# First projection in blocks of 2, 2, 4 and 8 k tiles, with the modulation placed anew

## The chip, the cores and the metric

One NeuronCore of a Trainium2 chip runs the kernel alone. TensorE (PE) multiplies matrices and holds its sums in PSUM, VectorE (DVE) and ScalarE (ACT) compute element by element, GpSimd (POOL) has little to do here, and SyncE (SP) issues most transfers from memory. The metric is the device time of one execution in microseconds.

## The reference

Two layers over 256 tokens of 2048 channels: layer 0 is gated linear attention (GLA), layer 1 a diagonal state-space mixer (S5). Each layer is modulated by a vector c, and its input is normalised after the residual:

```
mod = silu(c) @ ada_w + ada_b            # per layer: shift, scale, gate (2048 each)
u   = x * (1 + scale) + shift
# GLA
proj = u @ w_in                          # 2048 x (1024 q + 1024 k + 4096 v + 4096 z + 16 gate)
q, k, v, z, g = split(proj)
# per chunk of 64 tokens: state = decay * state + k_dec^T v ; o = q state
y = rmsnorm(o) * silu(z) ; h = y @ w_out
x = layernorm(alpha * x + (1 + gate) * h)
# S5: proj, per-group linear recurrence, gelu, GLU with a 4096 x 4096 matrix, output projection
```

All is float32. The change lies in the first projection (q, k and v of layer 0) and in the shift and scale of layer 0 that it needs.

## The kernel before

Channels are cut into 16 k tiles of 128. Each float32 product is made of three matmuls: weights are split into hi (a cast on ScalarE, L145) and lo (weight minus hi, on VectorE, L146), the input u likewise, and hi·hi, lo·hi and hi·lo are summed in PSUM (L167 to L169 for v, L180 to L182 for q and k).

The first projection can't begin with all 16 k tiles, since u needs shift and scale of the k tiles that it uses, and these are products of c with `ada_w` that have still to be loaded. So it runs over blocks of k tiles. In a block, `vqk_steps` (L366 to L401) takes a step for each column group of 512 (8 groups of v, 4 of q and k) and each pair of k tiles: load 512 KB of weights (`wload`, L136), `split`, then 12 matmuls of 128x512 for v or 24 of 128x256 for q and k. When a column group has all k tiles of the block, its sums leave PSUM: in block 0 by copies on ScalarE (L385, L399), later by additions on VectorE into `vbig` (L383) or `qk` (L397). The last block does q and k first. The four blocks have 2, 4, 4 and 6 k tiles: 12, 24, 24 and 36 steps.

A name such as lov33 is the lo of v, column group 3, k pair 3 (k tiles 6 and 7); v160 is the PSUM bank of group 1 in the block that begins at k tile 6, tokens 0 to 127.

Weights lie in a ring of 4 tiles and 2 borrowed ones, hi and lo in rings of 3. The transfers of weights, of modulation pieces and of x are all issued from SP's queue, in the order of the program.

Beside the steps runs other work, put there by a table (`put`, `put_ada`, `put_u`, L743 to L778): after step i of block n it issues the pieces listed for (n, i). A modulation piece `put_ada(part, k0, nk, dve, ...)` makes shift (part 0) or scale (part 1) of nk k tiles from k0: 4 loads of 1 MB for nk = 4, 4 groups of products, either on TensorE (`psa`, L272: 16 products) or, where dve is true, on VectorE (`row`, L264 and L266: 16 multiply-adds over 128 nk columns), and at the end small products that turn the row into columns (`psmod`, L236) and one VectorE operation that adds the bias (`mods`, L239 or L241). `put_u` transposes two k tiles of x on TensorE (`psx`, L357) and makes u from them (`uf`, `u0h`, `u0l`). Where the program orders it after a step, each piece is told to be issued after that step's lo and last matmul.

In block 2, a generator `lam` also computes the S5 layer's powers in small VectorE operations (`lamst`, `pwr`, `pwt`, `crci`), one portion a step, and `prep_small` fills a DRAM tensor with zeros (`dk<-zt`, L458). Powers are turned on TensorE (`psl`) and copied by ScalarE (`l8`, L574). In the last block, `pump(V_RATE)` runs a background list of tasks for layer 1's modulation and preparation, V_RATE tasks a step on average, and from step GATE_AT on the gate of the GLA is computed (`gla_gate`).

Before the first block, the head computes shift and scale for block 0's two k tiles at once (`ada_now`, L281 to L288). The order on each engine is set by a scheduler that takes these issue conditions and its own estimate of durations; the kernel does not write it out.

Of the kernel before, what the change touches and what calls it, by code (L numbers as in the profile page):

```python
# [16 lines left out]
D = 2048  # L17
# [16 lines left out]
def trunk(ctx, tc, x, c, ln_g, ln_b, ada_w, ada_b, gla_w_in, gla_gate_w2, gla_gate_b, gla_norm_g,  # L34
# [39 lines left out]
    def s8t(name, shape, dt=F32):  # L74
        return s8.tile([P] + shape, dt, tag="s8", name=name)
# [20 lines left out]
    def pump(rate=1.0):  # L96
        pace[0] += rate
        while pace[0] >= 1.0:
            pace[0] -= 1.0
            if bg:  # L100
                bg.pop(0)()
# [178 lines left out]

    def ada_now(*a, rows=None, between=None):  # L281
        loads, mults, fin = ada_pe(*a, rows=rows)
        for f_ in loads + mults[:-1]:
            f_()
        if between:
            between()
        mults[-1]()
        return fin  # L288

    gate_dst = [None, None]  # L290
# [45 lines left out]
    def x_load(c0, c1):  # L336
        if not xr:
            xr.extend([s8t(f"xrow{i}", [D]) for i in range(2)])
        for tt in range(2):
            dma(xr[tt][:, c0:c1], x[0, tt * P:(tt + 1) * P, c0:c1])  # L340
# [11 lines left out]
    def u_tr(k2):  # L352
        ps = psx(f"psx{k2}")
        for kk in range(2):
            for tt in range(2):
                k = k2 + kk
                PE.transpose(ps[:, kk * T + tt * P:kk * T + (tt + 1) * P], xr[tt][:, k * P:(k + 1) * P], ident)  # L357
        return ps

    def u_fin(k2, ps):  # L360
        for kk in range(2):
            k = k2 + kk
            uf = tp.tile([P, T], F32, tag="uf", name=f"uf{k}", bufs=2)
            V.tensor_scalar(uf, ps[:, kk * T:(kk + 1) * T], mods[:, 0, 1, k:k + 1], mods[:, 0, 0, k:k + 1], op0=ALU.mult, op1=ALU.add)
            hilo(u0.hi(k), u0.lo(k), uf)
# [42 lines left out]
    def vectors():  # L408
# [8 lines left out]
        S.copy(vt, ps[:, :104])  # L417

    ada0 = ada_now(0, 0, 0, 2)

    vr2 = tp.tile([64, P], F32, tag="vr2", name="vr2", bufs=1)
# [4 lines left out]
    PE.transpose(ps[:, :64], vr2, ident[:64, :64])  # L426
    S.copy(abT, ps[:, :64])

    blocks = ((0, 2), (2, 4), (6, 4), (10, 6))
    ada0()  # L430
    x_load(0, 256)
    early = more(2, 0)

    got = []
    ada_now(0, 1, *blocks[0], rows=[8, 4, 4], between=lambda: got.append(u_tr(0)))()
    u_fin(0, got[0])

# [222 lines left out]
    for part in range(2):  # L660
        for j in range(4):
            bg.extend(ada_dve(1, part, j))
    V_RATE, Z_RATE, OP_RATE = 0.825, 0.944, 0.755
    KEEP = (4, 6)
    GATE_AT = 15
    SCAN_RATE = 1.728
    Y_RATE = 2.311
    qt, kt = qk
# [77 lines left out]
    def put(n, i, f_):  # L746
        along.setdefault((n, i), []).append(f_)

    def put_ada(part, k0, nk, dve, at_load, at_mult, at_fin):
        loads, mults, fin = ada_pe(0, part, k0, nk, dve)  # L750
        for f_, at in zip(loads + mults + [fin], at_load + at_mult + [at_fin]):
            put(*at, f_)

    def put_u(k2, at_tr, at_fin):
        got = []
        put(*at_tr, lambda: got.append(u_tr(k2)))
        put(*at_fin, lambda: u_fin(k2, got[0]))

    def at(n, *i):
        return [(n, j) for j in i]  # L760

    put(0, 0, lambda: x_load(256, 768))
    put_ada(1, 2, 4, True, at(0, 0, 1, 2, 3), at(0, 1, 2, 3, 4), (0, 6))
    put_ada(0, 2, 4, False, at(0, 4, 5, 6, 7), at(0, 6, 6, 8, 8), (0, 9))
    put_u(2, (0, 10), (0, 10))
    put_u(4, (0, 11), (0, 11))
    put(1, 2, vectors)
    put_ada(1, 6, 4, True, at(1, 0, 2, 4, 6), at(1, 1, 3, 5, 7), (1, 9))
    put(1, 7, lambda: x_load(768, D))
    put_ada(0, 6, 4, False, at(1, 8, 10, 12, 14), at(1, 11, 11, 15, 15), (1, 17))  # L770
    put_u(6, (1, 19), (1, 19))
    put_u(8, (1, 21), (1, 21))
    put_ada(0, 10, 4, False, at(1, 16, 18, 20, 22), at(2, 0, 0, 2, 2), (2, 4))
    put_ada(1, 10, 4, False, at(2, 0, 2, 4, 6), at(2, 4, 4, 8, 8), (2, 10))
    put_ada(0, 14, 2, False, at(2, 8, 10), at(2, 12, 12), (2, 14))
    put_ada(1, 14, 2, False, at(2, 12, 14), at(2, 16, 16), (2, 18))
    for i, k2 in enumerate((10, 12, 14)):
        put_u(k2, (2, 19 + i), (2, 19 + i))  # L778

    for n, blk in enumerate(blocks):  # L780
        steps = vqk_steps(*blk)
        for i, f_ in enumerate(steps):
# [8 lines left out]
            elif n == 3:  # L791
                pump(V_RATE)
                if i >= GATE_AT:
                    next(gate, None)
# [89 lines left out]
    for g in range(8):  # L884
# [9 lines left out]
        for f in range(4):  # L894
            i = (g * 4 + f) % 8
# [354 lines left out]
    for g in range(8):  # L1250
# [9 lines left out]
        for f in range(4):  # L1260
            i = (g * 4 + f) % 8
# [43 lines left out]
    for g in range(8):  # L1305
# [14 lines left out]
        for f in range(4):  # L1320
            i = g * 4 + f
# [112 lines left out]
```

## Time and profile before

| | |
|---|---|
| median of 3 runs | 1849.08 us (1848.76 to 1849.77) |
| the profiled execution | 1845.55 us, span 1843.8 us, mean granted clock 0.994 |
| busy: TensorE / its weight loads | 1793.7 us (97%) / 1587.9 us (86%) |
| busy: VectorE / ScalarE / GpSimd | 1426.4 (77%) / 898.7 (49%) / 68.1 us (4%) |
| first projection, blocks 0 to 3 start at | 21.2, 76.1, 154.5, 241.2 us; it ends at 366.6 us |

The profile's times are from the start of the span. In lists of groups and instructions, "out<-in" names the tiles written and read; what stands in brackets, or behind a bar, is the idle time of the engine before the instruction and what ended it.

### The profile page before, as it was taken

Reading aid. Unit: us, or ns where it says so; the run is one execution under the profiler, and the core shown is the slowest. Engines: PE = TensorE matmul, PEld = TensorE weight load, DVE = VectorE, ACT = ScalarE, POOL = GpSimd, SP = SyncE. Lnnn points to the kernel's source line nnn. Section 1 sums busy time; section 2 is a strip of 40 time slices with the busy share of each in tenths; the row PEclk is TensorE's granted clock in tenths of the full one; section 3 lists DMA queues with packets and bytes.
Section 4 is the critical chain, followed back from the end, with each engine's and each line's share of the span. In section 5 each row is a group of like instructions: output and inputs, shape, how many; then the busy total and the mean of one; then the engine's idle time right before and its main releaser. Section 6 shows DMA issues by size and latency. Waiting matters only on the chain.

```text
span 1843.8 us, 33865 instructions
## 1 busy us (share of the span) xinstructions
PE 1793.7 (97%) x13619; PEld 1587.9 (86%) x13619; DVE 1426.4 (77%) x1890; ACT 898.7 (49%) x1252; POOL 68.1 (4%) x76
## 2 busy tenths in 40 slices
PE   6999999999999999999999999999999999999997
PEld 4777798799999888799999999989888888888885
DVE  4667875989999988697899789889677775557556
ACT  3533465655556333654544544545544544444332
POOL 0000000000000000002123210000000000000000
PEclk9999999999999999999999999999999999999999
DMA  9887976789889998575655477999688886668653
GB/s 354 321 319 251 326 230 213 219 296 325 285 277 325 336 353 287 172 221 158 178 156 150 138 211 213 240 246 249 223 275 268 274 277 208 190 192 326 193 184 92
DMA packets 244182, 449.48 MB, mean 244 GB/s; under 512 B 19540, under 2 KB 49678, under 8 KB 242742
## 3 DMA queue, kind: packets, MB, share of 16 engines
q1 hardware_dynamic: 240088, 437.86, 74.1%
q0 software_dynamic: 3168, 8.41, 1.6%
q8 instruction: 107, 1.75, 0.4%
q10 hardware_dynamic: 768, 1.05, 0.2%
q14 instruction: 51, 0.42, 0.1%
HBM read 432.81 MB, written 14.42 MB: 243 GB/s over the span
## 4 chain that ended last, share of the span: by engine, by line
PE 85%; DVE 8%; DMA 2%; ACT 2%; issue 2%; SPq 0%; DVEq 0%; ACTq 0%
PE gl L192 13%; PE gl L193 6%; PE op L168 6%; PE op L167 6%; PE op L169 6%; PE z L182 3%; PE z L180 3%; PE z L181 3%; PE sz L180 3%; PE v L168 3%; PE sz L181 3%; PE sz L182 3%; PE v L169 3%; PE v L167 3%; PE su L180 2%; PE su L182 2%
## 5 line engine op out<-in xcount | busy, mean ns | idle before, releaser
L146 DVE TENSOR_TENSOR logl<-wgl,higl 128x1024 fp32r<-128x1024 f32 x128 | 156.5, 1224 | 113.2 <-ACT higl L145 109.7
L145 ACT CAST higl<-wgl 128x1024 fp32r<-128x1024 f32 x128 | 134.5, 1052 | 170.0 <-PE gl L192 160.9
L192 PE MATMUL gl<-yp,higl 128*128 128x512 f32 x512 | 178.4, 393 | 0.1
L192 PE MATMUL gl<-yb,higl 128*128 128x512 f32 x512 | 178.3, 393 | 0.0
L145 ACT CAST hio<-wo 128x1024 fp32r<-128x1024 f32 x96 | 101.3, 1055 | 155.7 <-PE op L169 142.8
L146 DVE TENSOR_TENSOR loo<-wo,hio 128x1024 fp32r<-128x1024 f32 x96 | 117.3, 1223 | 65.0 <-ACT hio L145 63.0
L309 DVE SCALAR_TENSOR_TENSOR acc<-wa,cs,acc 128x512 f32<-128x512 f32 x215 | 160.5, 747 | 2.7
L180 PE MATMUL su<-u1h,hisu 128*128 128x256 f32 x512 | 153.4, 301 | 1.8 <-DVE vv L1082 1.8
L180 PE MATMUL sz<-u1h,hisz 128*128 128x256 f32 x512 | 149.7, 292 | 1.2 <-ACT zs L1264 1.2
L180 PE MATMUL z<-u0h,hiz 128*128 128x256 f32 x512 | 148.7, 290 | 0.0
L182 PE MATMUL su<-u1h,losu 128*128 128x256 f32 x512 | 145.6, 285 | 0.4 <-DVE losu L146 0.4
L182 PE MATMUL z<-u0h,loz 128*128 128x256 f32 x512 | 145.0, 283 | 0.9 <-DVE loz L146 0.9
L181 PE MATMUL su<-u1l,hisu 128*128 128x256 f32 x512 | 145.8, 285 | 0.0
L182 PE MATMUL sz<-u1h,losz 128*128 128x256 f32 x512 | 144.8, 283 | 0.2 <-DVE losz L146 0.2
L181 PE MATMUL sz<-u1l,hisz 128*128 128x256 f32 x512 | 144.7, 283 | 0.0
L181 PE MATMUL z<-u0l,hiz 128*128 128x256 f32 x512 | 144.7, 283 | 0.0
L193 PE MATMUL gl<-yb,logl 128*128 128x256 f32 x512 | 142.8, 279 | 0.0
L193 PE MATMUL gl<-yp,logl 128*128 128x256 f32 x512 | 141.6, 279 | 0.0
L145 ACT CAST hisz<-wsz 128x1024 fp32r<-128x1024 f32 x64 | 66.9, 1050 | 103.7 <-PE sz L181 58.3
L192 PEld LDWEIGHTS gl<-yp,higl 128*128 128x128 f32 x512 | 95.8, 187 | 22.1 <-issue 0.8
L192 PEld LDWEIGHTS gl<-yb,higl 128*128 128x128 f32 x512 | 95.9, 187 | 21.9
L145 ACT CAST hisu<-wsu 128x1024 fp32r<-128x1024 f32 x64 | 66.7, 1050 | 94.8 <-PE su L181 70.0
(321 smaller groups left out, 5022.5 us busy)
## 6 DMA issues: line engine op xcount, KB each, us to landing
wgl<-in_s_w_glu SPq DMA_DIRECT2D x128, 512.0 KB, 4.7
wa<-in_ada_w SPq DMA_DIRECT2D x115, 512.0 KB, 5.1
wv<-in_gla_w_in SPq DMA_DIRECT2D x64, 512.0 KB, 6.5
wz<-in_gla_w_in SPq DMA_DIRECT2D x64, 512.0 KB, 5.1
wsu<-in_s_w_in SPq DMA_DIRECT2D x64, 512.0 KB, 3.7
wsz<-in_s_w_in SPq DMA_DIRECT2D x64, 512.0 KB, 4.7
wo<-in_s_w_out SPq DMA_DIRECT2D x64, 512.0 KB, 4.6
a<-in_ada_w SPq DMA_DIRECT2D x31, 1024.0 KB, 9.7
```

The costliest lines, as they stand in the source:

```text
L145: S.copy(hi, w)
L146: last_lo[0] = V.tensor_tensor(lo, w, hi.bitcast(F32), op=ALU.subtract).ins
L167: PE.matmul(banks[tt], lhsT=uh, rhs=hi[:, kk, :], start=(k == first), stop=False)
L168: PE.matmul(banks[tt], lhsT=uh, rhs=lo[:, kk, :], start=False, stop=False)
L169: last_mm[0] = PE.matmul(banks[tt], lhsT=ul, rhs=hi[:, kk, :], start=False, stop=(k == last)).ins
L180: PE.matmul(o, lhsT=wh, rhs=u.hi(k), start=(k == first), stop=False)
L181: PE.matmul(o, lhsT=wh, rhs=u.lo(k), start=False, stop=False)
L182: last_mm[0] = PE.matmul(o, lhsT=wl, rhs=u.hi(k), start=False, stop=(k == last)).ins
L192: PE.matmul(banks[f], lhsT=hi[:, kk, fs], rhs=u.both(k), start=(k == 0), stop=False)
L193: PE.matmul(banks[f][:, :T], lhsT=lo[:, kk, fs], rhs=u.hi(k), start=False, stop=(k == last))
L309: V.scalar_tensor_tensor(acc[0], w[:, kk, :], cs[:, k:k + 1], acc[0], op0=ALU.mult, op1=ALU.add)
```

## The change

- The blocks have 2, 2, 4 and 8 k tiles: 12, 12, 24 and 48 steps, 96 as before.
- Of the modulation pieces, VectorE computes one of 2 k tiles (scale of tiles 2 and 3) instead of two of 4 k tiles (scale of 2 to 5 and 6 to 9); TensorE computes the others, in pieces of 4 but for shift of 2 and 3. Each piece stands at other steps.
- x comes in columns 0 to 256 in the head, 256 to 512 after the first step, 512 to 1024 in block 1, and the rest in block 2, instead of 256, 512 and 1280 columns.
- In the head, the transposes of x stand ahead of all products of the scale, not behind 12 of its 16 rows.
- V_RATE is 0.62 instead of 0.825, so that over 48 steps 29.8 tasks run (before 36 × 0.825 = 29.7); GATE_AT is 20 instead of 15.

```
--- before.py
+++ after.py
@@ -280,11 +280,12 @@
 
     def ada_now(*a, rows=None, between=None):
         loads, mults, fin = ada_pe(*a, rows=rows)
-        for f_ in loads + mults[:-1]:
+        for f_ in loads:
             f_()
         if between:
             between()
-        mults[-1]()
+        for f_ in mults:
+            f_()
         return fin
 
     gate_dst = [None, None]
@@ -426,7 +427,7 @@
     PE.transpose(ps[:, :64], vr2, ident[:64, :64])
     S.copy(abT, ps[:, :64])
 
-    blocks = ((0, 2), (2, 4), (6, 4), (10, 6))
+    blocks = ((0, 2), (2, 2), (4, 4), (8, 8))
     ada0()
     x_load(0, 256)
     early = more(2, 0)
@@ -660,9 +661,9 @@
     for part in range(2):
         for j in range(4):
             bg.extend(ada_dve(1, part, j))
-    V_RATE, Z_RATE, OP_RATE = 0.825, 0.944, 0.755
+    V_RATE, Z_RATE, OP_RATE = 0.62, 0.944, 0.755
     KEEP = (4, 6)
-    GATE_AT = 15
+    GATE_AT = 20
     SCAN_RATE = 1.728
     Y_RATE = 2.311
     qt, kt = qk
@@ -759,23 +760,24 @@
     def at(n, *i):
         return [(n, j) for j in i]
 
-    put(0, 0, lambda: x_load(256, 768))
-    put_ada(1, 2, 4, True, at(0, 0, 1, 2, 3), at(0, 1, 2, 3, 4), (0, 6))
-    put_ada(0, 2, 4, False, at(0, 4, 5, 6, 7), at(0, 6, 6, 8, 8), (0, 9))
+    put(0, 0, lambda: x_load(256, 512))
+    put_ada(1, 2, 2, True, at(0, 0, 1), at(0, 2, 3), (0, 5))
+    put_ada(0, 2, 2, False, at(0, 2, 4), at(0, 6, 6), (0, 8))
     put_u(2, (0, 10), (0, 10))
-    put_u(4, (0, 11), (0, 11))
-    put(1, 2, vectors)
-    put_ada(1, 6, 4, True, at(1, 0, 2, 4, 6), at(1, 1, 3, 5, 7), (1, 9))
-    put(1, 7, lambda: x_load(768, D))
-    put_ada(0, 6, 4, False, at(1, 8, 10, 12, 14), at(1, 11, 11, 15, 15), (1, 17))
-    put_u(6, (1, 19), (1, 19))
-    put_u(8, (1, 21), (1, 21))
-    put_ada(0, 10, 4, False, at(1, 16, 18, 20, 22), at(2, 0, 0, 2, 2), (2, 4))
-    put_ada(1, 10, 4, False, at(2, 0, 2, 4, 6), at(2, 4, 4, 8, 8), (2, 10))
-    put_ada(0, 14, 2, False, at(2, 8, 10), at(2, 12, 12), (2, 14))
-    put_ada(1, 14, 2, False, at(2, 12, 14), at(2, 16, 16), (2, 18))
-    for i, k2 in enumerate((10, 12, 14)):
-        put_u(k2, (2, 19 + i), (2, 19 + i))
+    put_ada(1, 4, 4, False, [(0, 6), (0, 8), (0, 10), (1, 0)], at(1, 0, 0, 2, 2), (1, 4))
+    put(1, 0, lambda: x_load(512, 1024))
+    put_ada(0, 4, 4, False, at(1, 1, 2, 4, 5), at(1, 5, 5, 8, 8), (1, 9))
+    put_u(4, (1, 10), (1, 10))
+    put_u(6, (1, 11), (1, 11))
+    put(2, 4, vectors)
+    put_ada(1, 8, 4, False, [(1, 7), (1, 9), (2, 0), (2, 1)], at(2, 0, 0, 3, 3), (2, 4))
+    put_ada(1, 12, 4, False, at(2, 2, 3, 5, 6), at(2, 6, 6, 8, 8), (2, 9))
+    put(2, 7, lambda: x_load(1024, D))
+    put_ada(0, 8, 4, False, at(2, 8, 9, 11, 12), at(2, 11, 11, 14, 14), (2, 15))
+    put_ada(0, 12, 4, False, at(2, 14, 15, 17, 18), at(2, 18, 18, 20, 20), (2, 21))
+    for i, k2 in enumerate((8, 10, 12, 14)):
+        at_ = (2, (17, 19, 22, 23)[i])
+        put_u(k2, at_, at_)
 
     for n, blk in enumerate(blocks):
         steps = vqk_steps(*blk)
```

What this does to the order is seen at three places. First TensorE in the head; `psa010` is the scale of k tiles 0 and 1, `psx0` the transposes of x for them, `psmod000` the shift's columns. Before:

```order
L236 MATMUL psmod000_147<-ones0_84,row000_138 128x1 x2
L272 MATMUL psa010_161<-a0100_155,cz_105 32x256 x8
L357 MATMUL psx0_174<-ident_89,xrow0_151 128x128
L357 MATMUL psx0_174<-ident_89,xrow1_152 128x128
L357 MATMUL psx0_174<-ident_89,xrow0_151 128x128
L357 MATMUL psx0_174<-ident_89,xrow1_152 128x128
L272 MATMUL psa010_161<-a0101_157,cz_105 32x256 x4
L272 MATMUL psa010_161<-a0102_159,cz_105 32x256 x4
```

And after:

```order
L236 MATMUL psmod000_147<-ones0_84,row000_138 128x1 x2
L358 MATMUL psx0_161<-ident_89,xrow0_151 128x128
L358 MATMUL psx0_161<-ident_89,xrow1_152 128x128
L358 MATMUL psx0_161<-ident_89,xrow0_151 128x128
L358 MATMUL psx0_161<-ident_89,xrow1_152 128x128
L272 MATMUL psa010_166<-a0100_155,cz_105 32x256 x8
L272 MATMUL psa010_166<-a0101_157,cz_105 32x256 x4
L272 MATMUL psa010_166<-a0102_159,cz_105 32x256 x4
```

The four transposes moved ahead of the scale's first eight rows.

Second VectorE in block 2, at column group 3 of v, whose first lo is `lov33` before and `lov32` after (the block's first k pair is 3 before and 2 after). `lamst` and `sm` belong to the S5 powers. Before:

```order
L383 TENSOR_TENSOR vbig_113<-vbig_113,v060_1323 128x512
L383 TENSOR_TENSOR vbig_113<-vbig_113,v061_1324 128x512
L146 TENSOR_TENSOR lov23_1458<-wv23_1455,hiv23_1457 128x1024
L488 TENSOR_TENSOR lamst_1354<-lamst_1354 128x128 x3
L146 TENSOR_TENSOR lov24_1498<-wv24_1495,hiv24_1497 128x1024
L535 RECIPROCAL lamst_1354<-lamst_1354 128x128
L383 TENSOR_TENSOR vbig_113<-vbig_113,v160_1381 128x512
L383 TENSOR_TENSOR vbig_113<-vbig_113,v161_1382 128x512
L146 TENSOR_TENSOR lov33_1539<-wv33_1536,hiv33_1538 128x1024
L464 TENSOR_SCALAR sm_1435<-sm_1435 128x2
```

And after:

```order
L474 TENSOR_SCALAR lamst_1054<-lamst_1054 128x128
L473 TENSOR_TENSOR lamst_1054<-lamst_1054 128x128
L384 TENSOR_TENSOR vbig_113<-vbig_113,v240_1157 128x512
L474 TENSOR_SCALAR lamst_1054<-lamst_1054 128x128
L473 TENSOR_TENSOR lamst_1054<-lamst_1054 128x128
L384 TENSOR_TENSOR vbig_113<-vbig_113,v241_1158 128x512
L474 TENSOR_SCALAR lamst_1054<-lamst_1054 128x128
L473 TENSOR_TENSOR lamst_1054<-lamst_1054 128x128
L146 TENSOR_TENSOR lov32_1243<-wv32_1240,hiv32_1242 128x1024
```

Before, the additions ahead of group 3's first lo are those of group 1 (`v160`, `v161`); after, they are those of group 2 (`v240`, `v241`).

Third ScalarE in block 2, at the copies of the last eight powers, `l8`, after:

```order
L145 CAST hiv52_1403<-wv52_1401 128x1024
L455 COPY dT_201<-psd_1348 16x256
L145 CAST hiv53_1427<-wv53_1425 128x1024
L575 ACTIVATE l8_200<-psl8_1484 128x2x64 x4
L145 CAST hiv62_1466<-wv62_1464 128x1024
L145 CAST hiv63_1523<-wv63_1521 128x1024
L145 CAST hiv72_1545<-wv72_1543 128x1024
L145 CAST hiv73_1575<-wv73_1573 128x1024
```

Before they stood behind the first cast of q:

```order
L145 CAST hiv73_1838<-wv73_1836 128x1024
L145 CAST hiv74_1862<-wv74_1860 128x1024
L275 COPY row0014_1773<-psa0014_1756 128x256
L145 CAST hiq03_1886<-wq03_1884 128x1024
L574 ACTIVATE l8_200<-psl8_1777 128x2x64 x4
L145 CAST hiq04_1935<-wq04_1933 128x1024
```

So they stand ahead of the cast of a step of v, `hiv62`, now, with `hiv62`, `hiv63`, `hiv72` and `hiv73` behind them.

## Rows read from the trace of the kernel before

**Rows 1.** The page, busy time of each engine.

```profile
PE 1793.7 (97%) x13619; PEld 1587.9 (86%) x13619; DVE 1426.4 (77%) x1890; ACT 898.7 (49%) x1252; POOL 68.1 (4%) x76
```

**Rows 2.** Windows of the first projection: PE, PEld, DVE, ACT, POOL busy, clock, DMA, GB/s.

```profile
21.20:32.30 11.10, 11.08 (x36) 8.03 (x36) 6.80 (x10) 5.24 (x8) 0.00 (x0) 1.00 1.05 387
32.30:41.00 8.70, 5.10 (x14) 3.47 (x14) 7.36 (x10) 3.39 (x5) 0.00 (x0) 0.80 1.05 387
41.00:54.20 13.20, 9.51 (x37) 6.21 (x37) 6.29 (x7) 5.38 (x9) 0.00 (x0) 1.00 1.05 387
54.20:76.10 21.90, 21.61 (x166) 17.51 (x165) 10.81 (x14) 14.71 (x29) 0.00 (x0) 1.00 0.73 243
98.30:105.00 6.70, 3.79 (x10) 2.86 (x10) 5.30 (x6) 0.84 (x1) 0.00 (x0) 0.75 1.05 387
154.50:241.20 86.70, 85.64 (x617) 66.96 (x616) 69.38 (x158) 33.12 (x46) 0.00 (x0) 1.00 0.84 280
241.20:366.60 125.40, 121.60 (x722) 104.32 (x723) 93.80 (x119) 81.27 (x86) 7.13 (x6) 1.00 0.74 226
366.60:1843.80 1477.20, 1452.36 (x11517) 1312.49 (x11517) 1169.85 (x1480) 722.25 (x1030) 60.29 (x64) 0.99 0.75 235
```

**Rows 3.** TensorE's waits from 140 to 245 us: total, times, longest.

```profile
PE v L167 <- ACT hiv L145: 0.7, 1, 0.7
PE v L168 <- DVE lov L146: 0.3, 1, 0.3
```

**Rows 4.** Timeline of TensorE: start, duration, instruction, idle before and what ended it.

```profile
13.60 1.93 PE L272 MATMUL psa<-a,cz 128*32 128x256 f32 x16 [0.52 <-DMA a<-in_ada_w]
...
36.60 0.80 PE L168 MATMUL v<-lov,u0h 128*128 128x512 f32 x1 [1.90 <-DVE lov L146]
...
50.50 0.73 PE L167 MATMUL v<-hiv,u0h 128*128 128x512 f32 x2 [1.62 <-ACT hiv L145]
51.76 0.50 PE L168 MATMUL v<-lov,u0h 128*128 128x512 f32 x1 [0.53 <-DVE lov L146]
...
101.42 0.80 PE L168 MATMUL v<-lov,u0h 128*128 128x512 f32 x1 [2.91 <-DVE lov L146]
102.02 0.63 PE L169 MATMUL v<-hiv,u0l 128*128 128x512 f32 x1
...
197.56 0.39 PE L169 MATMUL v<-hiv,u0l 128*128 128x512 f32 x1
...
200.20 0.50 PE L168 MATMUL v<-lov,u0h 128*128 128x512 f32 x1 [0.34 <-DVE lov L146]
```

**Rows 5.** The chain that ended last, 96 to 100 us: start, duration, what.

```profile
95.99 0.23 PE v L167
...
96.72 0.69 DVE vbig L383
```

**Rows 6.** Timeline of VectorE in block 2.

```profile
193.39 0.29 DVE L488 TENSOR_TENSOR lamst<-lamst 128x128 f32<-128x128 f32 x1
193.59 0.28 DVE L488 TENSOR_TENSOR pwt<-pwr 128x128 f32<-128x128 f32 x1
...
197.99 0.69 DVE L383 TENSOR_TENSOR vbig<-vbig,v 128x512 f32<-128x512 f32 x1
198.59 0.42 DVE L488 TENSOR_TENSOR pwr<-pwt 128x256 f32<-128x256 f32 x1
198.93 1.22 DVE L146 TENSOR_TENSOR lov<-wv,hiv 128x1024 fp32r<-128x1024 f32 x1
```

**Rows 7.** Groups from 20 to 370 us: busy and mean of one.

```profile
L145 ACT CAST hiv<-wv 128x1024 fp32r<-128x1024 f32 x63 | 66.1, 1050 | 82.9 <-PE v L169 60.5 <-PE q L181 8.5 <-DMA wv<-in_gla_w_in 7.2
...
L266 DVE SCALAR_TENSOR_TENSOR row<-a,cs,row 128x512 f32<-128x512 f32 x30 | 22.5, 749 | 0.6
...
L272 PE MATMUL psa<-a,cz 128*32 128x512 f32 x128 | 15.4, 598 | 0.0
```

**Rows 8.** ScalarE's copies of the powers in block 2.

```profile
210.61 0.79 ACT L574 ACTIVATE l<-psl 128x128 f32<-128x128 f32 x4 [1.23 <-PE psl L569]
```

## The prediction

> **What bounds the kernel now.** I read the page's busy shares first, then the windows of the first projection, then the waits, the timeline and the chain inside them. TensorE is busy for 97% of the span [rows 1]. So time can be won only where TensorE idles or does work that is not needed. After 366.6 us it works 1452.36 of 1477.20 us [rows 2], and nothing that the change touches lies there: that stretch is passed on unchanged. The prediction rests on the 367 us before it.
>
> Of these, the windows show three troubled stretches. From 32.3 to 54.2 us TensorE is busy 5.10 of 8.70 and 9.51 of 13.20 us, with the DMA engines full (share 1.05, 387 GB/s). From 98.3 to 105.0 us it is busy 3.79 of 6.70 us. The block from 154.5 to 241.2 us is nearly full (85.64 of 86.70 us), although VectorE is 80% busy there (69.38 us) [rows 2], and its waits are short, 0.7 and 0.3 us [rows 3].
>
> The causes of the first two can be followed. A step of a v group is 12 matmuls that start 0.23 us apart [rows 5], 2.74 us. Before a step can finish, ScalarE casts the weights to hi (1.05 us) [rows 7] and VectorE subtracts to get lo (1.22 us) [rows 6]. At 36.60 us TensorE had waited 1.90 us for a lo; at 50.50 and 51.76 us it waited 1.62 and 0.53 us; at 101.42 us 2.91 us, because VectorE had first to do an addition of 0.69 us, a modulation row of 0.75 and another addition [rows 4, 5, 7]. After the first and the last of these waits the granted clock falls, to 0.80 and 0.75 as means of their windows [rows 2]: a matmul lasts 0.63 us instead of 0.39 [rows 4], at the lower level, 1.2 GHz. At 50.50 us, after 1.62 us of wait, it stayed at 2.4 GHz. In the window from 98.3 us ten matmuls start; seven of them at half the pace cost 7 × 0.2 = 1.4 us.
>
> **The change part by part.** The sum is against the profiled execution's own 1845.55 us; the median of the runs is 1849.08, and I add the difference to that.
>
> *Head.* The four transposes of x (1.05 us in the chain of the head) now stand ahead of the scale's first eight rows, where TensorE waits 0.52 us for the scale's weights [rows 4]. They fill the wait and push the rest back by as much: −0.5 us.
>
> *Block 0.* It still has 12 steps of 2 k tiles, but the modulation pieces beside it are 2 tiles wide, not 4 (2 + 2 MB instead of 4 + 4), and x comes as 0.25 MB instead of 0.5. 4.25 MB at 387 GB/s are 11.5 us of a saturated queue [rows 2]. VectorE's modulation rows shrink from 0.75 us [rows 7] to about 0.46 (estimate: half the columns and the fixed part), so the lo at 36.60 comes about 2 us earlier. By window, TensorE loses about 2.9 us in the first (36 matmuls are 8.2 of 11.1 us), 5.5 in the second, 4.7 in the third and 2.2 in the fourth: 15.3. I leave the first 2.9, one wait like that of 50.50 and 51.76 us (2.15) and about 1 us of crumbs: 6.1. So −9.2 us. Bounds: nothing, if weights are limited by their ring rather than by the bytes, and −12.4, if only the first 2.9 stay.
>
> *Block 1.* It has 12 steps instead of 24, and no modulation rows on VectorE: the wait of 2.91 us with its 1.4 of half clock goes. VectorE is tighter, since in a block of 2 k tiles every step ends a column group: two additions and a lo, 2 × 0.60 + 1.22 = 2.4 of 2.74 us [rows 6]. Where the order puts a lo behind the additions of the step just done, products of modulation stand between on TensorE in all places but the first q group's second step, and there I take 1.0 us. −3.3 us; bounds −4.3 and 0.
>
> *Products.* Six columns of k tiles go from VectorE to TensorE. The four 4-wide pieces that TensorE made between 20 and 370 us kept it busy for 15.4 us [rows 7], 0.96 us a column: 6 × 0.96 = +5.8 us, all on the engine that sets the end, and certain to a few tenths. VectorE loses some 17 us, which were on the path only at the stretches counted above.
>
> *Block 2, the lo behind the additions.* Here the order matters. Before, in this block, lo of group 3 stands behind additions of group 1; now lo of group 3 stands behind the additions of group 2, the step just finished. The nearest row is the one place of before where this happens: the last matmul of the step at 197.56 ends at 197.95; the addition starts at 197.99, a piece of the power table at 198.59, the lo at 198.93, and TensorE goes on at 200.20 [rows 4, 6]. Less the 0.46 us of two hi matmuls that need no lo, this costs 0.04 + 0.60 + 0.34 + 1.22 + 0.05 − 0.46 = 1.8 us. In the new order, with 0.20 us for each small operation of the recipe between: the group 3 lo has two of them, 1.85 us; the group 4 lo three, 2.05; the group 5 lo a fill and the shift's or scale's add, of which products cover a part, 1.1; the first q, 0.7. Ahead of these, two steps of group 2 have 15 small operations between two lo's (3.0 us + 1.22 in a step of 2.74): 1.45 each, and 0.4 at group 3's second step. Sum 9.0; the 1.8 of before goes: +7.2 us. Bounds: −1, if VectorE arrives early as it did through all of this block before [rows 3], and +12, if each chain is like the 2.91 us [rows 4].
>
> *Group 6 of block 2.* The last eight powers are turned by TensorE between group 5 and group 6, and ScalarE's four pieces (0.79 us) [rows 8] now stand ahead of group 6's cast; before, no step of v stood behind them. 0.79 + 1.05 + 1.22 − 0.46 is 2.6, with handovers +2.8 us. Group 6's weight is issued behind the 1.8 MB zero fill; I hide its landing in this wait. Bounds 0 and +4.
>
> *Block 3 and the clock.* Eight k tiles give one group's additions per four steps instead of per three, on a VectorE less often in collision: TensorE loses 3.8 us there now [rows 2], −1.0 (0 to −2.6). And one of the new waits of 1.8 to 2.8 us, nearest to the two that dropped the clock (1.90, 2.91) and above the one that did not (1.62), drops it once: +1.4 (0 to +5.6).
>
> Sum: −0.5 − 9.2 − 3.3 + 5.8 + 7.2 + 2.8 − 1.0 + 1.4 = +3.2 us. The profiled execution would take about 1848.8 us and the median 1852.3.
>
> **The rivals.**
> *B, the lo chains are covered.* The price of block 2 rests on the written order, with TensorE early and VectorE at its heels. If VectorE is ahead, the additions are done half a step earlier and the lo is ready; before, this block at 80% VectorE had 1.0 us of waits in all [rows 2, 3]. Then the terms of block 2 and group 6 shrink from 10.0 to between −1 and 4 and the clock does not fall: −9.2 to −4.2, about 1842.5. It decides for "faster" as soon as these terms and the clock come to under 4.5 of their 11.4 us. Against it: the additions of the group just done wait for TensorE by data, which no early VectorE changes.
> *C, the clock falls at most of the new waits.* Five waits of about 2 us stand within some 25 us; three more falls of 1.4 and late weights behind the fill (+2) make +9, 1858. For it: it fell after 1.90 us [rows 4]; against it: it held at 50.50 us after 1.62 and 0.53, and through block 2 until now. [...]
> *D, the bytes taken away do not help.* The block's weights still pass rings of 6 and 3 tiles; if these set the pace in block 0, it keeps half of its loss: +4.6 more, about 1857. Against it: the queue is at 387 GB/s up to 54 us and falls to 243 only behind it, when the modulation pieces are through [rows 2].
>
> **How the numbers follow.** The forecast, A, gets 0.47 with its own range of 1848 to 1856; B 0.25; C 0.15; D 0.13. A change of 0.2%, 3.7 us, is what can be told from none: faster is below 1845.4, slower above 1852.8. B is below in four of five (0.20); A lies about half above 1852.8; with C and D slower gets 0.45, the same 0.35. For 8 in 10 the range takes half of B and half of C and D: 1843.5 to 1858.5.
>
> **What would show it.** Block 0 should end near 63 us, not 76, with no window of full DMA beyond about 45 us; if it ends past 70, D holds. No wait for a lo near 2.9 us should be left in block 1. In block 2, VectorE's lo for groups 3 and 4 should start right behind an addition that started at a step's end, and TensorE should wait over 1 us for each; if TensorE's waits in block 2 sum to under 4 us, B holds. Its wait for group 6's hi should end on the cast behind the four pieces. Windows of 2 us with a clock under 0.9 count the falls. From the first projection's end to the kernel's end the time should agree within 1 us; if not, the cause is one that I have not seen.

## The result, and the profile after

| | before | after |
|---|---|---|
| median of 4 runs each | 1849.42 us (1848.76 to 1850.50) | 1857.97 us (1856.20 to 1861.37) |
| ratio to before, 95% interval | | 1.0048 (1.0036 to 1.0061) |
| the profiled execution, span | 1845.55, 1843.8 us | 1856.20, 1854.4 us |
| first projection ends (first `psst` product) | 366.5 us | 379.1 us |

The change made the kernel 0.48% slower, 8.5 us by the medians. The page of the profile after, busy times of the engines, answers to [rows 1]:

```profile
PE 1801.8 (97%) x13651; PEld 1588.8 (86%) x13651; DVE 1414.5 (76%) x1874; ACT 898.5 (48%) x1253; POOL 69.1 (4%) x76
```

TensorE is 8.1 us busier, VectorE 11.9 us less busy. The windows of the projection answer to [rows 2]: first three steps of block 0, the wait at its fourth, the rest of it, blocks 1, 2 and 3, and all behind (length, then PE, PEld, DVE, ACT and POOL busy with their counts, clock, DMA share, GB/s):

```profile
19.84:30.60 10.76, 10.28 (x36) 7.71 (x36) 7.73 (x13) 5.17 (x9) 0.00 (x0) 0.84 1.09 355
30.60:38.00 7.40, 3.52 (x8) 2.31 (x9) 3.75 (x7) 2.65 (x3) 0.00 (x0) 0.77 1.07 371
38.00:64.92 26.92, 26.92 (x195) 23.47 (x193) 14.97 (x20) 20.11 (x37) 0.00 (x0) 1.00 1.05 386
64.92:112.70 47.78, 45.03 (x283) 33.60 (x281) 30.30 (x47) 13.97 (x17) 0.00 (x0) 1.00 0.89 313
112.70:219.79 107.09, 97.24 (x631) 70.60 (x630) 74.75 (x166) 34.32 (x49) 0.00 (x0) 0.95 0.81 280
219.79:379.06 159.27, 155.08 (x916) 134.00 (x914) 114.33 (x138) 94.80 (x101) 7.12 (x6) 1.00 0.71 222
379.06:1854.40 1475.34, 1453.20 (x11518) 1312.23 (x11517) 1166.02 (x1474) 722.24 (x1030) 61.24 (x64) 1.00 0.75 235
```

Block 2 is the place where the time was lost. Before, TensorE was busy for 85.64 of its 86.70 us [rows 2]; now for 97.24 of 107.09, at a mean clock of 0.95. The table has the lengths from block start to block start, and what is left over of them when the steps (2.74 us of v, 2.87 of q) and the modulation products, transposes and small products beside them, by the starts of TensorE's instructions at full clock, are taken off:

| | length before | after | left over before | after |
|---|---|---|---|---|
| block 0 | 54.6 | 45.1 | 15.1 | 8.7 |
| block 1 | 78.5 | 47.8 | 5.6 | 4.6 |
| block 2 | 86.7 | 107.1 | 4.2 | 19.7 |
| block 3 | 125.5 | 159.3 | 7.7 | 7.9 |

With the start, 1.4 us earlier, and 5.7 us more of products and other work beside the steps, -6.4 - 1.0 + 15.5 + 0.2 makes +12.6; the end of the projection moved by 12.55. Behind it the profile of after is 1.9 us shorter (1475.3 us against 1477.3).

TensorE's timeline after, the long waits (start, duration, instruction, idle before and what ended it), against [rows 4]:

```profile
34.26 1.03 PE L167 MATMUL v<-hiv,u0h 128*128 128x512 f32 x2 [3.72 <-ACT hiv L145]
...
78.89 0.73 PE L167 MATMUL v<-hiv,u0h 128*128 128x512 f32 x2 [1.65 <-ACT hiv L145]
...
133.99 0.50 PE L168 MATMUL v<-lov,u0h 128*128 128x512 f32 x1 [1.01 <-DVE lov L146]
...
138.95 0.50 PE L168 MATMUL v<-lov,u0h 128*128 128x512 f32 x1 [1.93 <-DVE lov L146]
...
150.54 0.79 PE L168 MATMUL v<-lov,u0h 128*128 128x512 f32 x1 [2.19 <-DVE lov L146]
...
161.96 0.50 PE L168 MATMUL v<-lov,u0h 128*128 128x512 f32 x1 [0.86 <-DVE lov L146]
...
172.33 0.73 PE L167 MATMUL v<-hiv,u0h 128*128 128x512 f32 x2 [2.65 <-ACT hiv L145]
173.59 0.50 PE L168 MATMUL v<-lov,u0h 128*128 128x512 f32 x1 [0.53 <-DVE lov L146]
```

The wait of 2.91 us at 101 us is gone. In block 2 four waits for a lo of v stand where one short one for a lo and one for a hi were [rows 3], and 2.65 us for the hi of group 6, with 0.53 for its lo. The chain behind the wait at 138.95 us, start, duration, what:

```profile
135.59 0.60 DVE vbig L384
...
136.65 0.65 DVE vbig L384
...
137.47 0.04 DVE lamst L473
...
137.68 1.23 DVE lov L146
...
138.95 0.50 PE v L168
```

It is the chain that the forecast added up: two additions of the step just done, pieces of the power recipe (`lamst`) between and behind them, and then the lo. For group 6's hi, ScalarE's timeline, then SP's, which issues the transfers, with SP's wait from 145 to 175 us (total, times, longest):

```profile
169.72 0.79 ACT L575 ACTIVATE l<-psl 128x128 f32<-128x128 f32 x4 [8.64 <-PE psl L570]
171.23 1.04 ACT L145 CAST hiv<-wv 128x1024 fp32r<-128x1024 f32 x1 [0.73 <-DMA wv<-in_gla_w_in]
```

```profile
155.73 0.37 SPq L254 DMA_DIRECT2D a<-in_ada_w  x1
160.78 0.92 SPq L459 DMA_DIRECT2D dk<-zt  x2
161.80 1.07 SPq L136 DMA_DIRECT2D wv<-in_gla_w_in  x1
```

```profile
SPq L459 <- DVE mods L241: 4.6, 1, 4.6
```

The copies of the powers end at 170.5 us, but the cast still waits 0.73 us for its weight. That weight is the transfer issued at 161.80, right behind the zero fill of 1.8 MB (`dk<-zt`). The fill had first held up SP's queue for 4.6 us: it needs a tile that VectorE clears from 160.32 to 160.75 us (the view names `mods`, the operation right behind), and until then nothing more was issued. So the weight left late, and the fill's bytes were on the way with it. And the clock, in 2 us windows behind four of these waits (columns as above):

```profile
36.00:38.00 2.00, 2.00 (x6) 1.52 (x6) 1.93 (x4) 0.00 (x0) 0.00 (x0) 0.52 1.04 383
142.00:144.00 2.00, 2.00 (x14) 0.48 (x16) 0.96 (x1) 0.66 (x1) 0.00 (x0) 0.57 0.39 144
152.00:154.00 2.00, 2.00 (x6) 1.61 (x5) 1.86 (x7) 0.00 (x0) 0.00 (x0) 0.51 0.13 45
176.00:178.00 2.00, 2.00 (x6) 1.16 (x4) 0.73 (x1) 1.49 (x2) 0.00 (x0) 0.54 1.04 385
```

At each of the four places TensorE is at 1.2 GHz for about 3 us. Before there were two such places, at 36 and 101 us. In both kernels the projection's first matmuls are at 1.2 GHz as well, 0.63 us each, until about 26 us before and 24 us after; the view's clock of 1.00 for 21.20 to 32.30 us before [rows 2] does not show this.

### The profile page after: what moved, and what is told of

Its sections match the earlier page's. It is cut to its first block, busy times and chain, and to the rows that moved or that the text cites. A ratio compares the mean times of both kernels' runs of the same rounds, so it can differ in the third digit from the quotient of the medians.

```text
span 1854.4 us, 33925 instructions
## 1 busy us (share of the span) xinstructions
PE 1801.8 (97%) x13651; PEld 1588.8 (86%) x13651; DVE 1414.5 (76%) x1874; ACT 898.5 (48%) x1253; POOL 69.1 (4%) x76
## 3 DMA queue, kind: packets, MB, share of 16 engines
q10 hardware_dynamic: 768, 1.05, 0.2%
## 4 chain that ended last, share of the span: by engine, by line
PE 81%; DVE 8%; DMA 5%; ACT 2%; issue 2%; SPq 1%; DVEq 0%; ACTq 0%
PE gl L192 13%; PE gl L193 7%; PE op L168 5%; PE op L169 5%; PE op L167 5%; PE sz L180 3%; PE sz L181 3%; PE sz L182 3%; PE z L182 3%; PE z L180 3%; PE z L181 3%; PE v L168 3%; PE v L169 3%; PE v L167 2%; PE su L180 2%; PE su L182 2%
## 5 line engine op out<-in xcount | busy, mean ns | idle before, releaser
L146 DVE TENSOR_TENSOR lov<-wv,hiv 128x1024 fp32r<-128x1024 f32 x64 | 77.9, 1220 | 49.0 <-ACT hiv L145 48.6
```

Source lines behind the costliest of these rows:

```text
L146: last_lo[0] = V.tensor_tensor(lo, w, hi.bitcast(F32), op=ALU.subtract).ins
```

## The experiments

The time behind the projection differs between profiles, from 1475.1 to 1482.3 us in the kernels whose code there is the same, most of it in the S5 layer's second projection (254.8 to 261.1 us). So the end of the projection in the profile tells the edits apart better than the medians. It is one profile for each kernel, though. Blocks with the same code agree between profiles within 0.2 us (block 0 takes 44.9 to 45.1 us in after, e1, e2, e3 and e5), but with the same head the first step begins anywhere from 19.5 to 20.2 us, and the clock can fall in one profile and not in the next: block 1 has the same waits of 1.65 and 0.53 us in after, e1 to e5 and e9, and takes 47.8 us, but 49.3 in e1 and 49.4 in e9, where the clock fell behind them at 81 to 82 us. So a difference of less than about 2 us between two of these ends says little by itself. All twelve:

| kernel | projection ends, us | median, us | ratio to before, 95% interval |
|---|---|---|---|
| before | 366.5 | 1847.4 to 1849.4 | 1 |
| after | 379.1 | 1857.97 | 1.0048 (1.0036 to 1.0061) |
| e1 additions behind the next lo | 377.0 | 1857.44 | 1.0052 (1.0037 to 1.0068) |
| e2 zero fill late | 373.0 | 1853.45 | 1.0031 (1.0020 to 1.0041) |
| e3 both | 370.9 | 1852.65 | 1.0024 (1.0013 to 1.0035) |
| e4 head as before | 379.4 | 1856.64 | 1.0053 (1.0037 to 1.0070) |
| e5 powers late | 382.1 | 1866.95 | 1.0097 (1.0080 to 1.0113) |
| e6 weights first | 380.5 | 1859.72 | 1.0065 (1.0051 to 1.0080) |
| e7 before, one piece to TensorE | 366.6 | 1846.44 | 0.9996 (0.9983 to 1.0010) |
| e8 e1, e2, e5, e6 together | 374.9 | 1857.25 | 1.0054 (1.0039 to 1.0068) |
| e9 casts first | 381.9 | 1862.85 | 1.0067 (1.0047 to 1.0087) |
| e10 casts and weights first | 374.8 | 1857.59 | 1.0048 (1.0034 to 1.0063) |
| e11 after, e1, e2, e10 | 369.9 | 1851.11 | 1.0019 (1.0006 to 1.0032) |
| e12 before, e1 and e9 | 363.1 | 1845.14 | 0.9983 (0.9971 to 0.9995) |

**e1, additions behind the next lo.** The additions of a finished group are kept and issued after the next step's `split`:

```
 w = split(wload(...))
+with tc.issue_after(last_lo[0]):
+    flush()                      # the kept additions
 mv_step(...)
...
-V.tensor_tensor(o, o, banks[cg][tt], op=ALU.add)
+pend.append(lambda ...: V.tensor_tensor(o, o, b, op=ALU.add))
```

> The kernel after, but the two additions of a finished v group are issued behind the lo of the next step. Theory A (order on VectorE): the waits of TensorE for a lo at groups 3, 4 and 5 of block 2 (2.08, 2.35 and 1.11 us of time each) shrink to under 1.5 us together, and the falls of the clock at 140 and 150 us go with them, so that it comes out 6 to 8 us faster than the kernel after, 1850 to 1852. Rival B (block 2 is short of VectorE or of transfers, whatever the order): the additions come later and the waits only move to the next steps; within 2 us of the kernel after, 1856 to 1860.

The projection's end moved by 2.1 us only. TensorE's timeline in block 2, the waits for a lo of v:

```profile
131.25 0.50 PE L168 MATMUL v<-lov,u0h 128*128 128x512 f32 x1 [0.49 <-DVE lov L146]
...
136.41 0.50 PE L168 MATMUL v<-lov,u0h 128*128 128x512 f32 x1 [1.08 <-DVE lov L146]
...
141.56 0.61 PE L168 MATMUL v<-lov,u0h 128*128 128x512 f32 x1 [2.10 <-DVE lov L146]
...
160.67 0.50 PE L168 MATMUL v<-lov,u0h 128*128 128x512 f32 x1 [1.02 <-DVE lov L146]
```

Group 4's wait of 2.19 us is gone, and the clock did not fall at 150 us. But at group 3's first step (141.56 us) 2.10 us stand where 1.93 stood, behind 1.08 at group 2's second: between these two lo's, where the additions were, VectorE does 16 pieces of the recipe, some 4 us. Block 2 is 4.2 us shorter, and block 1 is 1.5 us longer by the fall of the clock at 81 us told above, which the edit did not make: in e3, with the same additions in block 1, it did not fall. Theory A failed in its size: changing the order alone frees one of the waits.

**e2, the zero fill late**, and **e3, both**:

```
-                if i == 8:
-                    prep_small()
 ...
             elif n == 3:
                 pump(V_RATE)
+                if i == 0:
+                    prep_small()
```

> The kernel after, but the zero fill of 1.8 MB and the small preparation beside it stand in block 3, after its first step. Theory A (the fill delays group 6's weight in block 2, and with it hi and lo): the wait of 2.65 us for hi of group 6, the two waits for a lo behind it (0.53, 0.28) and the fall of the clock at 174 us go: 4 to 5 us faster than after, 1853 to 1854. Rival B (the copies of the powers ahead of that cast are what counts, as the forecast had it, or the 1 MB modulation loads): the wait stays at 2 us or more, and the time within 1.5 us of after.

> Both edits: additions behind the next step's lo, and the zero fill in block 3. If the two waits are separate, the gains add: 10 to 13 us faster than after, 1845 to 1848, at or below the kernel before. If they share a cause (VectorE or the queue of transfers is simply full in block 2), it is no better than the better of the two alone.

In e2 the end came 6.1 us earlier. TensorE's waits for a lo of v in its block 2 (total, times, longest):

```profile
PE v L168 <- DVE lov L146: 5.9, 4, 2.2
```

TensorE has no wait for a hi of v left in this block, and the clock does not fall at 174 us. SP now issues group 6's first weight some 6 us earlier than in the kernel after (161.80 there):

```profile
155.59 0.46 SPq L136 DMA_DIRECT2D wv<-in_gla_w_in  x1
```

Here the schedule also moved the copies of the powers behind group 7's first cast, so that e2 alone does not part the fill from the copies. e5 below does: there the powers and their copies are out of block 2, the fill is not, and group 6's wait stays, with the cast waiting for its weight. TensorE, then ScalarE, in e5:

```profile
166.17 0.73 PE L167 MATMUL v<-hiv,u0h 128*128 128x512 f32 x2 [2.57 <-ACT hiv L145]
```

```profile
165.07 1.04 ACT L145 CAST hiv<-wv 128x1024 fp32r<-128x1024 f32 x1 [9.44 <-DMA wv<-in_gla_w_in]
```

So the fill, with the small preparation that moved with it, makes this wait. Its hold on the queue and its bytes are not parted by a run. e3 ends 8.2 us earlier, as much as e1 and e2 together (2.1 + 6.1; 10 to 13 were expected, on e1's account). In part that is chance, since e1's end has the fall in block 1: in block 2 alone the gains of 4.2 and 5.7 us come to 8.3.

**e4, the head as before**:

```
-        for f_ in loads: f_()
-        between()
-        for f_ in mults: f_()
+        for f_ in loads + mults[:-1]: f_()
+        between()
+        mults[-1]()
```

> The kernel after, but with x's transposes again behind 12 of 16 rows of the scale's products. Theory A (the head's wait for the scale's weights is filled by the transposes): the first step of the projection begins 1.0 to 1.4 us later and the time is as much longer, 1859. Rival B (block 0 waits for weights at its fourth step anyway, so a head that is earlier only waits longer there): the fourth step begins at the same time and the end is the same within 0.5 us.

Rival B holds. The first step began 0.7 us later (20.50 against 19.84), which is little more than profiles with the same head differ by; the fourth began at 34.33 against 34.26, and the end moved by 0.3 us.

**e5, the powers late.** `next(lam)` runs in the first 24 steps of block 3, the background tasks at twice their rate behind.

> The kernel after, with the S5 layer's powers (small VectorE operations, one portion a step) moved from block 2 to the first 24 steps of block 3, and the background tasks of block 3 run at twice the rate in its last 24 steps. Theory A (block 2 is short of VectorE, because the powers meet a VectorE that comes out of block 1 without a lead; the order matters little): the waits for a lo between 133 and 162 us (1.0, 1.9, 2.2, 0.9) and the falls of the clock at 140 and 150 us go, block 2 is 8 to 11 us shorter, block 3 gives back up to 4; the projection ends at 370 to 374 us instead of 379.1. Theory B (the lo stands behind the additions of the step just done, and that chain is what costs): the chain is the same without the powers, each wait stays at 1.3 us or more, and the end moves by less than 4 us.

TensorE's timeline at groups 3 and 4:

```profile
137.33 0.50 PE L168 MATMUL v<-lov,u0h 128*128 128x512 f32 x1 [1.46 <-DVE lov L146]
...
146.65 0.50 PE L168 MATMUL v<-lov,u0h 128*128 128x512 f32 x1 [1.46 <-DVE lov L146]
```

VectorE at group 3:

```profile
134.30 0.69 DVE L384 TENSOR_TENSOR vbig<-vbig,v 128x512 f32<-128x512 f32 x1 [1.51 <-PE v L169]
135.45 0.69 DVE L384 TENSOR_TENSOR vbig<-vbig,v 128x512 f32<-128x512 f32 x1 [0.47 <-PE v L169]
136.06 2.35 DVE L146 TENSOR_TENSOR lov<-wv,hiv 128x1024 fp32r<-128x1024 f32 x2
```

Theory B holds at groups 3 and 4 (at groups 2 and 5 the waits are 0.82 us, under its 1.3): without the powers the chain is an addition and a lo behind the end of the step, and costs 1.46 us both times; the forecast's own terms without powers, 0.04 + 0.60 + 1.22 + 0.05 - 0.46, are 1.45. Theory A holds for the clock: behind waits of 1.46 us it did not fall. Block 2 was 100.4 instead of 107.1 us, but block 3 grew by 9.9 us (169.2), where the clock fell twice, and the stretch from the projection's end to the first product of z by 3.7 us. That VectorE is as short there is likely, but no run shows it apart from the doubled rate of the tasks.

**e6, the weights of block 0 first**:

```
-    put(0, 0, lambda: x_load(256, 512))
-    put_ada(1, 2, 2, True, at(0, 0, 1), at(0, 2, 3), (0, 5))
-    put_ada(0, 2, 2, False, at(0, 2, 4), at(0, 6, 6), (0, 8))
+    put(0, 3, lambda: x_load(256, 512))
+    put_ada(1, 2, 2, True, at(0, 2, 3), at(0, 5, 6), (0, 8))
+    put_ada(0, 2, 2, False, at(0, 4, 5), at(0, 7, 7), (0, 9))
```

> The kernel after, with the modulation loads and x of block 0 issued two or three steps later, behind more of the weights; their products stand later too. Theory A (the 3.7 us that TensorE waits at block 0's fourth step are two 1 MB modulation loads and x queued ahead of that weight): the wait is under 1 us, the fall of the clock behind it goes, and the projection ends 4 to 5 us earlier, 374 to 375. Rival B (the weight's ring tile comes free too late, the bytes do not matter): the wait stays above 2.5 us and the end moves by less than 1.5 us.

Neither holds. The fourth step began at 29.56 us without a wait, as Theory A had it, but from the fifth on new waits came. TensorE, then ScalarE:

```profile
34.06 0.73 PE L167 MATMUL v<-hiv,u0h 128*128 128x512 f32 x2 [1.62 <-ACT hiv L145]
35.32 0.50 PE L168 MATMUL v<-lov,u0h 128*128 128x512 f32 x1 [0.52 <-DVE lov L146]
...
39.51 0.73 PE L167 MATMUL v<-hiv,u0h 128*128 128x512 f32 x2 [1.62 <-ACT hiv L145]
```

```profile
32.48 0.58 ACT L386 COPY vbig<-v 128x512 f32<-128x512 f32 x1 [0.77 <-PE v L169]
32.96 1.05 ACT L145 CAST hiv<-wv 128x1024 fp32r<-128x1024 f32 x1
```

At the fifth step the cast to hi starts behind ScalarE's copy of the step just done, and 0.59 + 1.05 us (less the overlap, plus the handovers) are the 1.62 of TensorE's wait. Three such waits stand in block 0, and the same pattern is what TensorE shows before at 50.50 us [rows 4]. Block 0 is 4.7 us longer than in the kernel after (49.8), block 1 2.4 us shorter: the copies ahead of the cast are a second limit behind the late weight.

**e7, the kernel before with one piece on TensorE**: `put_ada(1, 6, 4, True, ...)` becomes False.

> The kernel before, with one modulation piece (scale of k tiles 6 to 9) made on TensorE instead of VectorE. Theory A (a column of products on TensorE costs 0.96 us on the path, and the VectorE rows cost only the wait of 2.91 us at 101 us with its half clock): + 3.9 - 2.9 - 1.4, the projection ends within 1 us of the kernel before (366.5). Rival B (the rows on VectorE were hidden but for this one wait, and something else ends the wait): it stays, +3.5 us or more.

Theory A holds: 366.6 against 366.5 us. The wait at 101 us and its half clock are gone, and the products cost as much. So at this place moving columns from VectorE to TensorE gains nothing, although VectorE is waited for.

**e8, e1, e2, e5 and e6 together.**

> The kernel after with all edits: additions behind the next lo, zero fill in block 3, powers in block 3, weights of block 0 first. If the causes are those of the profile (VectorE in block 2, the fill, the queue in block 0) the projection ends at 359 to 365 us, some 14 to 20 us before that of the kernel after and ahead of the kernel before (366.5); the whole 2 to 7 us under the kernel before. If what is moved out of block 2 only meets the same limit in block 3, it ends at 368 or later.

It ends at 374.9, past the 368 that would show the same limit in block 3. In block 2, TensorE's waits for a lo of v:

```profile
PE v L168 <- DVE lov L146: 1.6, 2, 0.8
```

For the lo's of groups 2 to 5, after waited 6.0 us in all, e1 (order) 4.7, e5 (no powers) 4.6, and with both 1.6. So the chain has two parts, the additions ahead of the lo and the powers around it, and taking away either alone leaves most of it. Block 2 is 91.8 us; block 3 keeps e5's loss (168.5).

**e9, casts first in block 0**, and **e10, casts and weights first.** The copies of a finished group are kept like e1's additions, and issued after the next step's cast (`tc.issue_after(last_hi[0])`).

> The kernel after; in block 0 ScalarE's two copies of a finished v group are issued behind the cast to hi of the next step (1.62 us of wait is a copy of 0.59 and a cast of 1.05). Theory A (at block 0's fourth step it is the weight that is late, its cast starts when it lands): the wait of 3.7 us stays within 0.7 us and the projection ends within 1 us of the kernel after, 378 to 380. Rival B (the copies ahead of the cast make it): under 2 us, the end 2 to 4 us earlier.

> The copies behind the next cast, and the weights of block 0 first, as in the run that delayed the modulation loads. Theory A (two limits in a row: take away the late weight and the copies ahead of the cast are next): the four waits of 1.62 us and the 0.5 us behind each, which that run showed, go too; block 0 is 4 to 7 us shorter than in the kernel after and the projection ends at 372 to 375. Rival B (the bytes are only paid later): the end stays above 378.

In e9 the wait at the fourth step was 4.26 us, as A said, but the end came 2.8 us later, not within 1. The clock accounts for it: after 3.72 us of wait in the kernel after it was back at 38 us, in e9 only between 40 and 42 (columns as above), and it fell once more at 82 us:

```profile
38.00:40.00 2.00, 2.00 (x6) 1.60 (x5) 1.86 (x5) 0.59 (x1) 0.00 (x0) 0.50 1.05 388
```

In e10 the waits of 1.62 us are gone and the end is 374.8 us, 4.3 before the kernel after. That is the end that A gave, but not by A's way: block 0, which should have been 4 to 7 us shorter, is 45.9 us, 0.9 longer than in the kernel after. The gain is in block 1 (2.4 us, as in e6) and in block 2 (2.6), where the clock fell once instead of three times, although TensorE's waits there are no shorter. What is left in block 0 are two waits of 0.53 us for a cast whose weight is late again and waits of 1.22 and 2.16 us for a lo, behind VectorE's modulation rows, which now stand between the steps:

```profile
43.10 4.12 DVE L266 SCALAR_TENSOR_TENSOR row<-a,cs,row 128x256 f32<-128x256 f32 x8
47.14 1.22 DVE L146 TENSOR_TENSOR lov<-wv,hiv 128x1024 fp32r<-128x1024 f32 x1
```

**e11, after with e1, e2 and e10**, and **e12, before with the two changes of order.**

> The kernel after with weights first and casts first in block 0, additions behind the next lo in the later blocks, and the zero fill in block 3. Sum of the single gains (5, 2, 6 us of the projection): it ends at 364 to 368, level with the kernel before (366.5); the whole within 3 us of the kernel before. If the gains share a cause, 369 or later.

> The kernel before with the two changes of order alone: copies of block 0 behind the next cast, additions behind the next lo. Theory A (the order costs in the old blocks too: waits of 1.62 us with 0.5 behind at 50 us, 1.0 at 45 us, 2.9 us with half a clock at 101 us): the projection ends at 361 to 364 instead of 366.5, and the kernel is 2 to 5 us faster than before. Rival B (these waits are VectorE's rows and the queue, whatever the order): within 1 us of 366.5.

e11 ends at 369.9, 9.2 us before the kernel after and still behind the kernel before: the single gains do not add, the case that was put at 369 or later. e12 ends at 363.1, 3.4 us before the kernel before, and is faster by 0.17% (0.05 to 0.29%): the only one of these kernels whose interval lies wholly below that kernel. TensorE, then VectorE, at what was the wait of 2.91 us:

```profile
97.19 0.50 PE L168 MATMUL v<-lov,u0h 128*128 128x512 f32 x1 [1.14 <-DVE lov L146]
```

```profile
92.89 3.11 DVE L266 SCALAR_TENSOR_TENSOR row<-a,cs,row 128x512 f32<-128x512 f32 x4
95.92 1.22 DVE L146 TENSOR_TENSOR lov<-wv,hiv 128x1024 fp32r<-128x1024 f32 x1
97.05 1.28 DVE L391 TENSOR_TENSOR vbig<-vbig,v 128x512 f32<-128x512 f32 x2
```

With the additions behind the lo, what remains is 1.14 us, for the four modulation rows that still stand ahead. The edit has a price of its own, too: blocks 0 and 1 are 3.0 and 2.6 us shorter, but block 2 is 2.3 us longer. There the kept additions of the last v group are issued ahead of the first q step, its cast starts when they end, and the clock fell behind the wait. TensorE, then ScalarE:

```profile
208.85 0.39 PE L180 MATMUL q<-u0h,hiq 128*128 128x256 f32 x1 [1.82 <-ACT hiq L145]
```

```profile
207.76 1.04 ACT L145 CAST hiq<-wq 128x1024 fp32r<-128x1024 f32 x1 [3.50 <-DVE vbig L391]
```

## Why the prediction was right or wrong

The forecast was 1852.3 us, 3.2 above before. The time moved the way that was forecast, but by more: 8.5 us by the medians, 10.7 between the two profiles. The measured 1857.97 us lies 0.5 us inside the forecast's wide range, and outside of its own 1848 to 1856. The missing 7.5 us are mostly the clock (2.9), block 0 (2.8) and block 1 (2.3). The time is that of rival C (1858), and both of C's causes, more falls of the clock and a weight late behind the fill, are a part of the reason.

- **Products** (+5.8): 5.5 by the starts of the matmuls, 0.93 us a column. Right; e7 shows the exchange against VectorE's rows at nothing gained.
- **Block 2's chains and group 6** (+7.2 and +2.8): the leftover grew by 15.5 us, of which the three falls of the clock at 140, 150 and 174 us are about 1.4 us each by the matmuls' late starts. That leaves some 11 against 10.0. Single waits, with their handovers by the starts of matmuls: 1.27 us at group 2's second step (1.45 forecast), 2.08 at group 3 (1.85), 2.35 at group 4 (2.05), 1.11 at group 5 (1.1). The mechanism held at these places, and e5 gives the price without the powers, from the end of the last matmul as the forecast counted it, as 1.46 us against 1.45. That the sum came so near is in part luck: at group 2's first step and group 3's second, where 1.45 and 0.4 were forecast, there is no wait, and at the first q 0.33 us instead of 0.7, while group 6's three waits make 3.46 us instead of 2.8.
- **Its cause at group 6**: the copies ahead of the cast were to be the limit and the weight's landing hidden behind them. It was the other way round, by 0.73 us. e2 without the fill has no such wait, and e5 without the copies has it (2.57 us): the fill, with the small preparation beside it, is the cause. That it holds up SP's queue while it waits for VectorE was not thought of.
- **The clock** (+1.4): the term that was missed most. Three falls in block 2 instead of one, +4.3, and the fall at 36 us, which the term of block 0 had taken as gone, stayed. That is C's mechanism, at its number of falls. As the clock fell at one and the same wait in one profile and not in another, this number is not fixed by the waits alone.
- **Block 0** (-9.2): -6.4. Its bytes did fall, but the fourth step's weight landed no earlier (its cast starts at 33.16 us, against 32.86 before): SP issued it at 21.20 us, behind three modulation loads that held SP for 7.8 us, and at 18.21 us before, where three held it for 4.7. The wait there is 3.72 us, where 2.15 had been left, and the clock fell behind it. The queue stayed full to 68 us, not to 45. Rival D is not borne out by its own sign either: the block ended at 64.9 us, not past 70, and is 9.5 us shorter. In e6 and e10 the late weight is gone, and then ScalarE's copies, later weights and VectorE's rows are waited for: in the four kernels with its loads moved (e6, e8, e10, e11) the block takes 45.9 to 50.0 us, none less than the 45.1 of the kernel after.
- **Block 1** (-3.3): -1.0. The wait at 101 us went (the forecast's account of it leaves out two more modulation rows, 1.53 us from 98.70 us, ahead of the lo), but at 78.89 and 80.15 us there are 1.65 and 0.53 new ones: the cast stands behind ScalarE's copy of a modulation row, and the forecast had not looked for a wait of this kind on ScalarE.
- **Head** (-0.5): the start came 1.4 us earlier and, by e4, is worth 0.3 at the end, no more than profiles differ by, because the fourth step waits for its weight in any case.
- **Block 3** (-1.0): +0.2.
- **Behind the projection** (0 within 1 us): -1.9, within what that part varies by among kernels that do not differ there.
- **Rival B** (chains covered) falls: the additions wait for TensorE by data, as was held against it, and TensorE's waits in block 2 come to 9.8 us, where under 4 would have shown B.

## What to carry to other kernels

When a tuned kernel's work is cut anew, look at what each in-order engine does between the end of one step and the operand of the next: an evacuation of the finished step ahead of the next step's cast or subtraction puts both on the path, 1.46 and 1.62 us here. Block 2 of the kernel before hid it, where the additions ahead of a lo were those of a group further back. (An evacuation is the copy or addition that takes a finished sum out of PSUM.) Telling the scheduler to issue the evacuation behind the next operand was worth 3.4 us of the projection in the old kernel, more than the new cut in any form tried, although it cost 2.3 us in one block; look at each place. Look also for a transfer that waits for an engine in a queue that weights share: here a zero fill held it for 4.6 us. Count stalls of two engines and the clock together: one that is freed shows the next, and a wait can bring another 1.4 us of half clock. And check a gain stage by stage: e10 ended where it was expected to, by gains in other blocks than the one that was edited.

## What the runs showed of the hardware

The length of a single wait did not tell whether the clock falls. It fell behind waits of 1.93, 2.19, 2.65 and 3.72 us in the kernel after; it held behind 2.16 us in e10 (48.41 us) and 2.20 us in e10 (113.95 us), and fell behind 2.15 us at the same place of e11 (48.20 us) and in e11 behind 1.08 us (134.18 us). Waits that are the same to 0.01 us, 1.65 and 0.53 us in block 1, were followed by a fall in e1 (81 us) and e9 (82 us) and by none in after, e2, e3, e4 and e5; and 2.20 us at block 2's first step, behind which it held in e10, were followed by a fall in e6 (117.47 us). A fall cost about 1.4 us where it lasted 3 us, and in e9 it lasted twice as long. What decides it stays open here.
